# Hybrid attention and gMLP block on one core: the closing norm of the MLP's last eight blocks, worked half a row at a time

## The chip, the core and the metric

The kernel runs on one core of a Trainium2 chip. The metric is device microseconds of that core for one launch. Five engines work beside each other, each through its own queue in order: TensorE (PE in the profile, with its weight loads as PEld), VectorE (DVE), ScalarE (ACT), GpSimd (POOL) and SyncE (SP), which here only issues transfers.

## What is computed

The reference is one decoder layer on 2048 rows of 1024 channels, in float32: a norm, dilated window attention and a gated spatial mixer, their merge, a projection, a norm added to the input; then a squared-ReLU MLP with a norm before and after it. Only the very end matters here:

```python
def _rmsnorm(x, gain):
    xf = x.astype(jnp.float32)
    y = xf * lax.rsqrt(jnp.mean(xf * xf, axis=-1, keepdims=True) + EPS)
    return (y * gain.astype(jnp.float32)).astype(x.dtype)
...
h = _rmsnorm(x, norm_pre_mlp[layer])
a = jax.nn.relu(jnp.einsum('bsd,df->bsf', h, w_mlp_in[layer]))
y = jnp.einsum('bsf,fd->bsd', a * a, w_mlp_out[layer])
x = x + _rmsnorm(y, norm_post_mlp[layer])
```

So every row of y needs its sum of squares over 1024 channels, the reciprocal root of their mean, a product with the gain (`gfin`), a product with the root, and a sum with the row of x that went into the MLP (`x1`).

## The kernel before

**Tiles and stages.** Each float32 operand is split into a rounded high part and the rest (`split`, L70 for the high part, L78 for the rest), and each product is three matmuls (high-high, high-rest, rest-high). The second product of the MLP is the last stage, from 2139.5 us on. It runs over 64 steps n (`ysteps`): eight groups of the 4096 inner channels, and in each group eight blocks of 256 rows. Steps 56 to 63 are the last group, in which every block gets its final sums. A block is two parts of 128 rows (ci = 0 and 1), each with two halves of 512 channels (h = 0 and 1): four quarters (ci, h), which lie in two accumulators of 128 x 1024 (`acc`).

**Products.** A block is multiplied by a 2 x 2 scheme with seven products instead of eight, numbered 1, 2, 6, 7, 5, 4, 3 in their order (`yproduct`, L1529 and L1534). One product is six matmuls of 128x512. Products 1, 6, 7 and 4 collect in one bank (a), 2 in its own (b), 5 and 3 in a third (c). After each one VectorE adds the bank so far to a quarter (L1534), and the next product of the bank waits for that add. The quarters are complete after product 2 (quarter 0,0), 5 (1,1), 4 (1,0) and 3 (0,1). Three blocks of the last group (`PLAIN`) are multiplied plainly instead: eight products p0 to p7, two for each quarter, one add for each two (L1512 and L1516). In the text below "58's product 6" is product 6 of step 58.

**The order.** A list (`yorder`) lays the products of neighbouring steps into each other: in the window of step n stand, in this order, n's 1, (n-1)'s 7 and 5, n's 2 and 6, (n-1)'s 4 and 3. A plain block puts p0 to p3 in its window and p4 to p7 in the next. The other four engines do their work in the order in which the code issues it; nothing is rearranged. Behind the last product of step n (L1597) the sums and splits of step n+3's left operand begin (`sum_s`): a first split (ACT, then DVE), four sums on POOL (L1330 to L1333), and one and two windows' slots later a second and a third split. A plain step has only two splits, the second with its rest on POOL.

**The closing norm.** `finish(n)` starts right behind the last product of step n of the last group. It issues four loads of `x1` on SP's queue (L1438) into four places of their own, then four squares on ACT, each with a sum over 512 channels (L1442), and four products with the gain on POOL (L1443). Three slots later comes the reciprocal root (`rstd_act`, L119 to L129: nine small steps on ACT and one reciprocal on DVE), and at six and seven slots two and two instructions on DVE that multiply by the root and add `x1` (L1449), each followed by its store (L1450). The last step has its own functions (`finish_half`, `finish_row`, `load_final`); its `x1` goes into the two accumulators of step 56, and those four loads are issued behind the last product of step 62 ahead of step 62's own. At the very end stand a chain on DVE and ACT for the last 128 rows (L1480, `rstd_of` L102 to L113, L1487) and two stores.

Two late loads (L1588) bring two more quarters of the MLP's weights (`w2r_b`) for the plain blocks; they wait until POOL has read the buffers that they reuse, and are split on ACT and DVE (L1591).

Of the kernel before, what the change touches and what calls it, by code (L numbers as in the profile page):

```python
# [16 lines left out]
P = 128  # L17
S = 2048
D = 1024
# [22 lines left out]
def block_kernel(ctx, tc, a, out):  # L42
# [73 lines left out]
    def rstd_act(pl, ss, n, scale, tag):  # L116

        b, w, v, r, t = (pl.tile([P, n], F32, name=f"{o}_{tag}", tag=f"ra_{o}{n}") for o in "bwvrt")
        act.activation(b, ss[:, 1], AF.Identity, bias=eps, scale=scale)  # L119
# [3 lines left out]
        act.activation(w, v, AF.Copy, scale=-0.5)  # L123
        dve.reciprocal(r, r)
        act.activation(t, r, AF.Square)
        for k in range(n):
            act.activation(t[:, k:k + 1], t[:, k:k + 1], AF.Identity, bias=three_halves, scale=w[:, k:k + 1])
        for k in range(n):
            act.activation(r[:, k:k + 1], r[:, k:k + 1], AF.Copy, scale=t[:, k:k + 1])  # L129
        return r  # L130

    def dtile(shape, name):
        return dram.tile(shape, F32, name=name)
# [1296 lines left out]
    def finish(n):  # L1430

        g, half, i = ysteps[n]
        ss = sm.tile([P, 2, 2], F32, name=f"fs_{n}", tag="fs")
        rows = [(ci, h, half * HALF + ci * 512 + i * P, slice(h * 512, (h + 1) * 512)) for ci in range(2) for h in range(2)]
        x1 = {}
        for ci, h, t0, nsl in rows:
            x1[ci, h] = rx.tile([P, 512], F32, name=f"x1_{n}{ci}{h}", tag="xs", bufs=LEAD + 1)
            sp.dma_start(x1[ci, h], x1_d[t0:t0 + P, nsl])  # L1438
        for ci, h, t0, nsl in rows:
            junk = psum_any(f"jk_{n}{ci}{h}")  # L1440
            y = acc[half, i, ci][:, nsl]
            act.activation(junk, y, AF.Square, accum_out=ss[:, h, ci:ci + 1])  # L1442
            pool.tensor_mul(y, y, gfin[h])  # L1443
        yield
        r = rstd_act(sm, ss, 2, 1.0 / D, f"fin{n}")
        yield
        for m, (ci, h, t0, nsl) in enumerate(rows):
            y = acc[half, i, ci][:, nsl]
            dve.scalar_tensor_tensor(y, y, r[:, ci:ci + 1], x1[ci, h], op0=OP.mult, op1=OP.add)  # L1449
            sp.dma_start(out[t0:t0 + P, nsl], y)  # L1450
            if m == 1:
                yield

    fin_ss, fin_x1, fin_y, last_rows = {}, {}, {}, {}

    def finish_half(ci, h):

        n = FINAL
        g, half, i = ysteps[n]
        if not h:  # L1460
            fin_ss[ci] = sm.tile([P, 2, 1], F32, name=f"fe_{ci}", tag=f"fe{ci}")
        y = acc[half, i, ci][:, h * 512:(h + 1) * 512]
        junk = psum_any(f"jk_{n}{ci}{h}")
        act.activation(junk, y, AF.Square, accum_out=fin_ss[ci][:, h])
        fin_y[ci, h] = y
        if h:

            z = acc[blocks[1] + (ci,)][:, :512]
            fin_y[ci, h] = z
            dve.tensor_mul(z, y, gfin[h])  # L1470
        else:
            pool.tensor_mul(y, y, gfin[h])

    def finish_row(ci):
        n = FINAL
        g, half, i = ysteps[n]
        t0 = half * HALF + ci * 512 + i * P
        ss = fin_ss[ci]
        if ci:
            dve.tensor_add(ss[:, 0], ss[:, 0], ss[:, 1])  # L1480
            r = rstd_of(sm, ss[:, 0], 1, 1.0 / D, f"fin{n}{ci}")
        else:
            r = rstd_act(sm, ss, 1, 1.0 / D, f"fin{n}{ci}")
        yield
        for h in range(2):
            y, nsl = fin_y[ci, h], slice(h * 512, (h + 1) * 512)
            dve.scalar_tensor_tensor(y, y, r, fin_x1[ci, h], op0=OP.mult, op1=OP.add)  # L1487
            (act if ci and h else sp).dma_start(out[t0:t0 + P, nsl], y)
        yield

    def load_final():
        n = FINAL
        last_rows.update((ci, finish_row(ci)) for ci in range(2))
        g, half, i = ysteps[n]
        for ci, h in OUTPUTS:
            t0 = half * HALF + ci * 512 + i * P
            x1 = acc[blocks[0] + (ci,)][:, h * 512:(h + 1) * 512]
            sp.dma_start(x1, x1_d[t0:t0 + P, h * 512:(h + 1) * 512])
            fin_x1[ci, h] = x1

    def plain(n, k):

        g, half, b = ysteps[n]
        (ci, nh), t = OUTPUTS[k // 2], k % 2
        if not t:
            ybank[n, k // 2] = psum_any(f"y{k // 2}_{n}")
        p = ybank[n, k // 2]
        at_, name = ((0, 1), (3, 2))[ci][t], (("B11", "B21"), ("B12", "B22"))[nh][t]
        for m, q in enumerate((2 * g, 2 * g + 1)):
            s, w = st_[n][:, :, m, at_], w2_[q, name]  # L1510
            for o, (l, r) in enumerate(((0, 0), (0, 1), (1, 0))):
                pe.matmul(p, s[:, l], w[:, r], start=not t and not m and not o, stop=t == 1 and m == 1 and o == 2,  # L1512
                          skip_group_check=True)
        if t:
            an = acc[half, b, ci][:, nh * 512:(nh + 1) * 512]
            dve.tensor_add(an, an, p)  # L1516

    def yproduct(n, i):

# [32 lines left out]
    def at(k, gen):  # L1552
        todo.setdefault(k, []).append(gen)
# [4 lines left out]
    for k, (_, n, i) in enumerate(yorder):  # L1558
# [25 lines left out]
        if (n, i) == (PLAIN[0] - 3, 3):  # L1584

            for q in (NQ - 2, NQ - 1):
                w2r_[q] = r4.tile([P, 5, 512], F32, name=f"w2r_b{q}", tag="w2r", bufs=2)
                sp.dma_start(w2r_[q][:, 1], a["w_mlp_out"][2 * q][:, 512:])  # L1588
        if (n, i) == (PLAIN[0] - 2, 7):
            for q in (NQ - 2, NQ - 1):  # L1590
                op_w2(q, "B12", "dve")  # L1591
        if n == FINAL:
            if i[1] % 2:
                finish_half(*OUTPUTS[i[1] // 2])
            for at_, ci in ((4, 0), (6, 0), (7, 1), (7, 1)):
                if i[1] == at_:
                    next(last_rows[ci])  # L1597
        elif i in (3, ("p", 7)):
            m = n + 3
            if m < len(ysteps):  # L1600
# [3 lines left out]
                load_s(m + 1)  # L1604
                at(k + 6, st)
                at(k + 7, st)
            if n == FINAL - 1:
                load_final()
# [74 lines left out]
```

## Time and profile before

| | us |
|---|---|
| three timed runs | 2808.26, 2811.08, 2811.70 (median 2811.08) |
| profiled execution | 2814.08 |
| span of its instructions | 2812.4 |
| TensorE busy | 2722.6 (97%) |
| VectorE, ScalarE, GpSimd busy | 1568.7, 1061.8, 976.7 |
| granted TensorE clock, mean | 0.987 |

Times in the profile count from the first instruction of the span. A row of the timeline has the start, the length, engine, source line, operation, output and inputs by the program's names without buffer numbers, how many instructions it merges, and in brackets the idle time ahead of it with what ended it. A row of the list of waits has who waited for whom, the sum, the number of waits and the longest. In the profile `s` is the split left operand, `sraw` its raw form, `jk` the thrown-away output of a square, `T_spots` split weights, `x` a place for `x1`, and `acc`, `acc_yt`, `acc_gmlp`, `B_acc`, `acc_y`, `acc_xr` are the accumulators of the blocks in the order of the steps.

### The profile page before, as it was taken

How to read it: one execution, taken by the hardware profiler on the slowest of the kernel's cores; microseconds unless marked ns; L12 is line 12 of the kernel's file. 1: busy time of each engine (PE TensorE's matmuls, PEld its weight loads, DVE VectorE, ACT ScalarE, POOL GpSimd, SP SyncE). 2: the span in 40 equal slices, each digit the busy share in tenths (PEclk: the TensorE clock that was granted, in tenths of full speed). 3: DMA queues.
4: the chain of work that ended last, by engine and by line, in shares of the span. 5: the costliest groups of instructions: out<-in, count | busy, mean ns of one | idle time of the engine just before them, and what ended most of it. 6: DMA issues, size and time to landing. Idle time of an engine off the chain costs nothing.

```text
span 2812.4 us, 36260 instructions
## 1 busy us (share of the span) xinstructions
PE 2722.6 (97%) x13382; PEld 2280.1 (81%) x13382; DVE 1568.7 (56%) x2670; ACT 1061.8 (38%) x2164; POOL 976.7 (35%) x806
## 2 busy tenths in 40 slices
PE   8999999999999999999998999999999999999987
PEld 8889888988878888787787788888887778877765
DVE  5664552433443344555556644655437777777767
ACT  4212111244444322344444545655444323332334
POOL 0241341200000023312215423233224777666765
PEclk9999999999999999999999999999999999999998
DMA  7544455466666554555658433643443221222235
GB/s 252 178 147 162 158 152 186 129 183 196 197 218 191 176 174 139 182 194 158 179 172 282 145 116 120 208 144 119 121 127 100 88 79 57 83 83 85 88 101 200
DMA packets 298673, 426.61 MB, mean 152 GB/s; under 512 B 18560, under 2 KB 172416, under 8 KB 298496
## 3 DMA queue, kind: packets, MB, share of 16 engines
q1 hardware_dynamic: 210800, 373.17, 42.0%
q10 hardware_dynamic: 87696, 51.13, 6.0%
q8 instruction: 105, 1.72, 0.3%
q14 instruction: 72, 0.59, 0.1%
HBM read 283.52 MB, written 140.71 MB: 151 GB/s over the span
## 4 chain that ended last, share of the span: by engine, by line
PE 79%; POOL 8%; DVE 4%; DMA 4%; issue 2%; ACT 2%; SPq 1%; ACTq 0%; DVEq 0%; POOLq 0%
PE ab L993 9%; PE ya L1529 7%; PE ac L993 6%; PE aa L993 5%; POOL T_spots L78 4%; PE g L95 4%; PE g L97 4%; PE g L96 4%; PE yc L1529 4%; PE x L97 3%; PE x L96 3%; PE x L95 3%; PE o L97 2%; PE o L95 2%; PE o L96 2%
## 5 line engine op out<-in xcount | busy, mean ns | idle before, releaser
L1529 PE MATMUL ya<-T_spots,s 128*128 128x512 f32 x1377 | 341.4, 394 | 5.0 <-DVE acc L1537 3.0
L1529 PEld LDWEIGHTS ya<-T_spots,s 128*128 128x128 f32 x1377 | 259.9, 189 | 64.5 <-issue 5.4
L70 ACT ACTIVATE s<-sraw 128x768 fp32r<-128x768 f32 (+1 forms) x189 | 130.0, 699 | 376.2 <-POOL sraw L1331 207.2
L993 PE MATMUL aa<-B,A 128*128 128x512 f32 x768 | 187.1, 396 | 7.3 <-ACT xs L1007 5.6
L78 DVE TENSOR_TENSOR s<-sraw,s 128x512 fp32r<-128x512 f32 (+1 forms) x181 | 177.6, 1003 | 29.8 <-ACT s L70 29.5
L1529 PE MATMUL yc<-T_spots,s 128*128 128x512 f32 x684 | 181.3, 396 | 10.5 <-DVE acc L1534 6.2
L964 POOL TENSOR_TENSOR s<-w1r 128x512 f32<-128x512 f32 x32 | 43.5, 1361 | 395.1 <-DVE S L78 335.1
L993 PEld LDWEIGHTS aa<-B,A 128*128 128x128 f32 x768 | 145.4, 190 | 41.3 <-ACT xs L1007 6.0
L72 POOL TENSOR_SCALAR w_g<-w_g_r 128x1024 fp32r<-128x1024 f32 x32 | 33.6, 1049 | 411.6 <-PE g L97 352.5
L1529 PEld LDWEIGHTS yc<-T_spots,s 128*128 128x128 f32 x684 | 127.8, 189 | 44.2 <-POOL T_spots L78 11.1
L95 PE MATMUL x<-hT_a,wq 128*128 128x512 f32 x384 | 149.7, 390 | 0.0
L97 PE MATMUL x<-hT_a,wq 128*128 128x512 f32 x384 | 149.4, 389 | 0.0
L96 PE MATMUL x<-hT_a,wq 128*128 128x512 f32 x384 | 149.4, 389 | 0.0
L630 DVE TENSOR_REDUCE o<-po 128x256 f32<-128x512 f32 x48 | 33.2, 691 | 183.9 <-PE po L629 183.9
L78 POOL TENSOR_TENSOR T_spots<-w2r,T_spots 128x512 fp32r<-128x512 f32 x92 | 131.8, 1460 | 0.0
L70 ACT ACTIVATE hl<-r 128x512 fp32r<-128x512 f32 x48 | 30.4, 633 | 231.5 <-POOL r L275 86.7
L1330 POOL TENSOR_TENSOR sraw<-sraw 128x256 f32<-128x256 f32 x61 | 45.0, 738 | 186.5 <-DVE s L78 172.2
L95 PE MATMUL o<-wo,mg 128*128 128x512 f32 x256 | 101.4, 396 | 4.7 <-ACT mg L70 4.2
L95 PE MATMUL g<-hT_b,w_g 128*128 128x512 f32 x256 | 105.3, 412 | 0.0
L95 PE MATMUL g<-hT_a,w_g 128*128 128x512 f32 x256 | 104.8, 409 | 0.0
L792 POOL TENSOR_TENSOR g<-g,g 128x512 f32<-128x512 f32 x28 | 38.9, 1388 | 186.2 <-DVE g L790 186.0
L70 ACT ACTIVATE S<-w1r 128x512 fp32r<-128x512 f32 x96 | 60.0, 629 | 113.9 <-PE ac L993 68.1
(381 smaller groups left out, 7447.2 us busy)
## 6 DMA issues: line engine op xcount, KB each, us to landing
w1r<-in_w_mlp_in_dram SPq DMA_DIRECT2D x64, 512.0 KB, 3.7
sraw<-sd SPq DMA_DIRECT2D x128, 256.0 KB, 3.4
qk<-hl SPq DMA_DIRECT2D x24, 1024.0 KB, 5.3
qq<-qk SPq DMA_DIRECT2D x96, 256.0 KB, 4.9
w_g_r<-in_w_in_dram SPq DMA_DIRECT2D x32, 512.0 KB, 5.5
gated<-gt SPq DMA_DIRECT2D x64, 256.0 KB, 3.0
g<-gated SPq DMA_DIRECT2D x64, 256.0 KB, 4.4
w2r<-in_w_mlp_out_dram SPq DMA_DIRECT2D x16, 1024.0 KB, 5.7
```

The costliest lines, as they stand in the source:

```text
L70: act.activation(hi, src, AF.Copy)
L72: pool.tensor_scalar(hi, src, 1.0, 1.0, op0=OP.mult, op1=OP.mult)
L78: (pool if lo_eng == "pool" else dve).tensor_sub(lo, src, f32(hi))
L95: pe.matmul(ps, lh, rh, start=start, stop=False)
L96: pe.matmul(ps, lh, rl, start=False, stop=False)
L97: pe.matmul(ps, ll, rh, start=False, stop=stop)
L630: dve.tensor_reduce(ot[:, :, j * 64:(j + 1) * 64], po.rearrange("p (b h e) -> p b e h", b=4, h=2), axis=AX.X, op=OP.add)
L792: (dve if dt == KT - 1 else pool).tensor_add(parts[0], parts[0], parts[1])
L964: pool.tensor_add(s1, a21, a22)
L993: pe.matmul(p, w[:, l, k, :], h[:, r, k, :], start=i in (1, 6, 5) and not k and not n, stop=k == 3 and n == 2, skip_group_check=True)
L1330: pool.tensor_add(a22, a21, a22)
L1529: pe.matmul(p, s[:, l], w[:, r], start=i in (1, 2, 5) and not m and not o, stop=m == 1 and o == 2, skip_group_check=True)
```

## The change

Each quarter's square and product with the gain are issued at once behind the add that completes it (`end_half`), in plain blocks after p1, p3, p5 and p7. `finish(n)` keeps only the reciprocal root, whose first part (up to the square root) is now issued one slot behind the block's last product and the rest one slot later, and the two pairs of closing instructions, at four and five slots. Their order in a block of seven products is (0,0), (1,1), (1,0), (0,1). `x1` is loaded behind the first completed quarter of its own block: for step 56 into places of its own, for 57 and 58 into the unused parts of the two late weight buffers, and for n from 59 on into the accumulators of step n-3, once these are stored. The plain blocks are now 59, 61 and 63 instead of 58, 60 and 63. The split of the two late weight quarters stands one step later.

```diff
+        yield r
         dve.reciprocal(r, r)
...
-    PLAIN = [n for n in range(len(ysteps)) if n >= len(ysteps) - len(blocks) and n % len(blocks) in (2, 4, 7)]
+    PLAIN = [n for n in range(len(ysteps)) if n >= len(ysteps) - len(blocks) and n % len(blocks) in (3, 5, 7)]
...
+    def load_x1(n):
+        for ci, h, t0, nsl in places_of(n):
+            if n == FIRST_END:
+                t = rx.tile([P, 512], F32, name=f"x1_{n}{ci}{h}", tag="xs", bufs=LEAD + 1)
+            elif n < FIRST_END + 3:
+                t = wb_[n - FIRST_END - 1][:, (0, 2, 3, 4)[2 * ci + h]]
+            else:
+                t = acc[blocks[n - FIRST_END - 3] + (ci,)][:, nsl]
+            sp.dma_start(t, x1_d[t0:t0 + P, nsl])
...
+        act.activation(junk, y, AF.Square, accum_out=ss_[n][:, h, ci:ci + 1])
+        if n == FINAL and h:
             z = acc[blocks[1] + (ci,)][:, :512]
             dve.tensor_mul(z, y, gfin[h])
+            y = z
         else:
             pool.tensor_mul(y, y, gfin[h])
...
+        rows = [rows[k] for k in ((0, 1, 2, 3) if n in PLAIN else (0, 3, 2, 1))]
+        for k in (0, 2):
+            end(n, r, 0, rows[k:k + 2], (sp, sp))
+            yield
...
             dve.tensor_add(an, an, p)
+            end_half(n, ci, nh)
...
+        if n >= FIRST_END and i in (2, 5, 4, 3):
+            end_half(n, ci, nh)
...
-        if (n, i) == (PLAIN[0] - 2, 7):
+        if (n, i) == (FIRST_END + 1, 7):
             for q in (NQ - 2, NQ - 1):
                 op_w2(q, "B12", "dve")
+        if n >= FIRST_END and i in (2, ("p", 0)):
+            load_x1(n)
...
-                next(f)
-                for d in (1, 3, 4) if n == FINAL - 1 else (3, 6, 7):
+                at(k + 1, f)
+                for d in (2, 3, 4) if n == FINAL - 1 else (2, 4, 5):
```

Lines after the first hunk stand higher by one to six in the changed kernel (L1534 becomes L1537, L1449 becomes L1471). The order of every engine is the same in both programs up to step 56.

**ACT, around the splits for step 62.** `s_62` and `s_63` are the split operands of those steps, `jk_6010` is the square of quarter (1,0) of step 60. Before:

```order
L1442 ACTIVATE jk_5911_22296,fs_59_22278<-acc_yt4_17862 128x512
L127 ACTIVATE t_fin59_22325<-t_fin59_22325,edge_87,w_fin59_22322 128x1 x2
L129 ACTIVATE r_fin59_22324<-r_fin59_22324,t_fin59_22325 128x1 x2
L70 ACTIVATE s_62_22268<-sraw_62_22166 128x2x256
L70 ACTIVATE s_62_22268<-sraw_62_22166 128x2x2x128
L70 ACTIVATE s_63_22385<-sraw_63_22275 128x2x256
L1442 ACTIVATE jk_6000_22397,fs_60_22388<-acc_yt5_17863 128x512
L1442 ACTIVATE jk_6001_22400,fs_60_22388<-acc_yt5_17863 128x512
L1442 ACTIVATE jk_6010_22403,fs_60_22388<-B22_acc_17855 128x512
L1442 ACTIVATE jk_6011_22406,fs_60_22388<-B22_acc_17855 128x512
```

And now:

```order
L1458 ACTIVATE jk_6011_22339,fs_60_22249<-B22_acc_17855 128x512
L1458 ACTIVATE jk_6100_22350,fs_61_22349<-B22_acc_17855 128x512
L1458 ACTIVATE jk_6010_22375,fs_60_22249<-B22_acc_17855 128x512
L70 ACTIVATE s_62_22287<-sraw_62_22183 128x2x256
L1458 ACTIVATE jk_6001_22387,fs_60_22249<-acc_yt5_17863 128x512
L70 ACTIVATE s_62_22287<-sraw_62_22183 128x2x2x128
L70 ACTIVATE s_63_22392<-sraw_63_22294 128x2x256
L1458 ACTIVATE jk_6101_22402,fs_61_22349<-B22_acc_17855 128x512
L119 ACTIVATE b_fin60_22405<-fs_60_22249,edge_87 128x2
L121 ACTIVATE v_fin60_22407<-fs_60_22249,b_fin60_22405 128x1 x2
```

The second and third split for step 62 stood together, ahead of all four squares of step 60; now each stands behind a square of step 60, that of the quarter which product 4 or 3 of step 60 completes, and the square of quarter (0,1) stands between the two.

**DVE, the same place.** `yc_60` and `ya_60` are the banks of step 60, and an L1537 row with `ya_62` is the add of 62's product 1. Now:

```order
L1471 SCALAR_TENSOR_TENSOR acc_yt3_17861<-acc_yt3_17861,r_fin59_22307,acc1_17856 128x512 x2
L1471 SCALAR_TENSOR_TENSOR acc_yt4_17862<-acc_yt4_17862,r_fin59_22307,acc0_17702 128x512 x2
L1537 TENSOR_TENSOR B22_acc_17855<-B22_acc_17855,ya_60_22206 128x512
L78 TENSOR_TENSOR s_62_22287<-sraw_62_22183,s_62_22287 128x2x256
L1537 TENSOR_TENSOR acc_yt5_17863<-acc_yt5_17863,yc_60_22331 128x512
L78 TENSOR_TENSOR s_62_22287<-sraw_62_22183,s_62_22287 128x2x2x128
L78 TENSOR_TENSOR s_63_22392<-sraw_63_22294,s_63_22392 128x2x256
L1518 TENSOR_TENSOR B22_acc_17855<-B22_acc_17855,y1_61_22357 128x512
L1537 TENSOR_TENSOR B22_acc_17855<-B22_acc_17855,ya_62_22415 128x512
L125 RECIPROCAL r_fin60_22408<-r_fin60_22408 128x2
```

The four closing instructions of step 59 stand ahead of the add for 60's product 4, and behind that add the rests of three splits alternate with adds, up to the add for 62's product 1, for which 62's product 6 waits. Before, the same add stood behind the rests of the splits and step 59's closing instructions as well, but no rest there came behind a square of that window.

**DVE, at the end.** `y3_63` is the bank of the last two products. Before:

```order
L124 RECIPROCAL r_fin62_22621<-r_fin62_22621 128x2
L1470 TENSOR_TENSOR acc_yt0_17857<-acc_y11_17865,gfin1_17852 128x512
L124 RECIPROCAL r_fin630_22647<-r_fin630_22647 128x1
L1516 TENSOR_TENSOR acc_xr0_17866<-acc_xr0_17866,y2_63_22637 128x512
L1449 SCALAR_TENSOR_TENSOR B22_acc_17855<-B22_acc_17855,r_fin62_22621,x1_6200_22591 128x512
L1449 SCALAR_TENSOR_TENSOR B22_acc_17855<-B22_acc_17855,r_fin62_22621,x1_6201_22593 128x512
L1449 SCALAR_TENSOR_TENSOR acc_y10_17864<-acc_y10_17864,r_fin62_22621,x1_6210_22595 128x512
L1449 SCALAR_TENSOR_TENSOR acc_y10_17864<-acc_y10_17864,r_fin62_22621,x1_6211_22597 128x512
L1487 SCALAR_TENSOR_TENSOR acc_y11_17865<-acc_y11_17865,r_fin630_22647,acc1_17856 128x512
L1487 SCALAR_TENSOR_TENSOR acc_yt0_17857<-acc_yt0_17857,r_fin630_22647,acc1_17856 128x512
L1516 TENSOR_TENSOR acc_xr0_17866<-acc_xr0_17866,y3_63_22672 128x512
```

And now:

```order
L1462 TENSOR_TENSOR acc_yt0_17857<-acc_y11_17865,gfin1_17852 128x512
L125 RECIPROCAL r_fin62_22600<-r_fin62_22600 128x2
L1518 TENSOR_TENSOR acc_xr0_17866<-acc_xr0_17866,y2_63_22607 128x512
L1471 SCALAR_TENSOR_TENSOR B22_acc_17855<-B22_acc_17855,r_fin62_22600,acc_yt3_17861 128x512
L1471 SCALAR_TENSOR_TENSOR acc_y10_17864<-acc_y10_17864,r_fin62_22600,acc_yt4_17862 128x512
L125 RECIPROCAL r_fin630_22623<-r_fin630_22623 128x1
L1471 SCALAR_TENSOR_TENSOR acc_y10_17864<-acc_y10_17864,r_fin62_22600,acc_yt4_17862 128x512
L1471 SCALAR_TENSOR_TENSOR B22_acc_17855<-B22_acc_17855,r_fin62_22600,acc_yt3_17861 128x512
L1471 SCALAR_TENSOR_TENSOR acc_y11_17865<-acc_y11_17865,r_fin630_22623,acc_yt5_17863 128x512
L1471 SCALAR_TENSOR_TENSOR acc_yt0_17857<-acc_yt0_17857,r_fin630_22623,acc_yt5_17863 128x512
L1518 TENSOR_TENSOR acc_xr0_17866<-acc_xr0_17866,y3_63_22647 128x512
```

The instructions are the same ones, in nearly the same places; what moved is their second input. Step 62's `x1` is now in the accumulators of step 59 (`acc_yt3`, `acc_yt4`), loaded a window and more ahead, where it was in `x1_62` places whose loads are issued behind the last stores. On SP the loads of `x1` for step 63 stood just ahead of those for step 62 and behind the stores of steps 60 and 61:

```order
L1450 DMA out_0_dram<-B22_acc_17855 128x512 x4
L1498 DMA acc1_17856<-x1d_79 128x512 x2
L1498 DMA acc0_17702<-x1d_79 128x512 x2
L1438 DMA x1_6200_22591<-x1d_79 128x512
L1438 DMA x1_6201_22593<-x1d_79 128x512
```

Now they stand behind the stores of step 60 alone:

```order
L1472 DMA out_0_dram<-acc_yt5_17863 128x512
L1448 DMA acc_yt3_17861<-x1d_79 128x512 x2
L1448 DMA acc_yt4_17862<-x1d_79 128x512 x2
L1448 DMA acc_yt5_17863<-x1d_79 128x512 x2
L1448 DMA B22_acc_17855<-x1d_79 128x512 x2
L1472 DMA out_0_dram<-B22_acc_17855 128x512 x5
```

What moved is the stores of step 61, now behind these loads.

More of the change, by code (lines that the diff above doesn't have):

```diff
@@ L1428, in block_kernel, with places_of @@
     begun, ybank, left, todo = set(), {}, {}, {}
-    def finish(n):
+    FIRST_END = len(ysteps) - len(blocks)
+    x1_, ss_, y_, wb_, last_rows = {}, {}, {}, {}, {}
+    def places_of(n, ci=None):
         g, half, i = ysteps[n]
[L1433 to L1452, printed above, removed]
@@ L1454, in block_kernel @@
-    fin_ss, fin_x1, fin_y, last_rows = {}, {}, {}, {}
-    def finish_half(ci, h):
-        n = FINAL
+        return [(c, h, half * HALF + c * 512 + i * P, slice(h * 512, (h + 1) * 512)) for c in range(2) for h in range(2)
+                if ci in (None, c)]
+    def load_x1(n):
[7 more added lines that the diff above has]
+            sp.dma_start(t, x1_d[t0:t0 + P, nsl])
+            x1_[n, ci, h] = t
@@ L1474, in finish_row, with finish @@
+    def finish(n):
+        r_ = rstd_act(sm, ss_[n], 2, 1.0 / D, f"fin{n}")
+        r = next(r_)
+        yield
+        next(r_)
+        yield
+        rows = places_of(n)
+        rows = [rows[k] for k in ((0, 1, 2, 3) if n in PLAIN else (0, 3, 2, 1))]
+        for k in (0, 2):
+            end(n, r, 0, rows[k:k + 2], (sp, sp))
+            yield
     def finish_row(ci):
         n = FINAL
-        g, half, i = ysteps[n]
-        t0 = half * HALF + ci * 512 + i * P
-        ss = fin_ss[ci]
+        ss = ss_[n][:, :, ci:ci + 1]
@@ L1482, in finish_row @@
         else:
-            r = rstd_act(sm, ss, 1, 1.0 / D, f"fin{n}{ci}")
-        yield
[L1485 to L1499, printed above, removed]
+            r_ = rstd_act(sm, ss, 1, 1.0 / D, f"fin{n}{ci}")
+            r = next(r_)
+            yield
+            next(r_)
+            yield
+        end(n, r, ci, places_of(n, ci), (sp, act if ci else sp))
+        yield
     def plain(n, k):
```

33 lines of the change are left out of this document (17 added, 16 removed).

## The prediction

> **What bounds the kernel now.** First the page's totals, then for the last stretch the list of waits, the windows with the granted clock, and the timeline.
>
> ```profile
> span 2812.4 us, 36260 instructions
> PE 2722.6 (97%) x13382; PEld 2280.1 (81%) x13382; DVE 1568.7 (56%) x2670; ACT 1061.8 (38%) x2164; POOL 976.7 (35%) x806
> ```
>
> TensorE sets the time everywhere, and up to step 56 the programs agree. So only the last 126 us can change: the last group's 63 products, and what follows them. TensorE's timeline (start, length, line, what, and in brackets the idle time ahead with its releaser) at the first of them, and at two that wait:
>
> ```profile
> 2686.38 2.90 PE L1529 MATMUL ya<-T_spots,s 128*128 128x512 f32 x12
> ...
> 2711.67 2.93 PE L1529 MATMUL yc<-T_spots,s 128*128 128x512 f32 x6 [6.20 <-DVE acc L1534]
> ...
> 2773.51 1.65 PE L1529 MATMUL ya<-spot,s 128*128 128x512 f32 x3 [4.71 <-DVE B_acc L1534]
> ```
>
> The list of waits from 2660 to the end (sum, number, longest) has four for TensorE that count, and two that stand behind the first:
>
> ```profile
> PE yc L1529 <- DVE acc L1534: 6.2, 1, 6.2
> PE ya L1529 <- DVE B_acc L1534: 4.7, 1, 4.7
> PE ya L1529 <- DVE acc_yt L1534: 2.7, 1, 2.7
> PE yc L1529 <- POOL T_spots L78: 0.7, 1, 0.7
> ACT T_spots L70 <- DMA w2r_b<-in_w_mlp_out_dram: 10.2, 2, 8.7
> DVE T_spots L78 <- ACT T_spots L70: 7.3, 2, 5.9
> ```
>
> The 6.2 is 56's product 3, the 2.7 is 59's product 6 and the 4.7 is 62's product 6. Each costs more than its length. The windows behind the three waits and the last stretch (window: length, then busy time and instructions of PE, PEld, DVE, ACT and POOL, granted clock, DMA):
>
> ```profile
> 2711.70:2717.00 5.30, 5.30 (x13) 4.14 (x14) 3.35 (x5) 2.37 (x6) 0.86 (x2) 0.50 0.62 189
> 2735.00:2743.50 8.50, 8.46 (x24) 6.69 (x25) 5.56 (x10) 2.93 (x8) 1.27 (x1) 0.63 0.85 297
> 2773.50:2778.80 5.30, 5.29 (x13) 4.14 (x14) 2.59 (x5) 2.60 (x10) 2.46 (x3) 0.50 0.57 172
> 2778.80:2797.40 18.60, 18.31 (x79) 14.37 (x77) 13.49 (x19) 11.07 (x40) 12.33 (x9) 1.00 0.59 208
> ```
>
> In the last window 79 matmuls take 18.31, so one product of six takes 1.37 with its share of overlap. At a clock of 0.50 half of 5.3 is lost, 2.65, and at 0.63 it is 0.37 x 8.5 = 3.1. Losses: 6.2 + 2.65, 2.7 + 3.1, 4.7 + 2.65, 0.7, about 23; with 63 x 1.37 = 86.3 and small waits the products end at 2797.4. The tail:
>
> ```profile
> 2791.59 5.79 PE L1512 MATMUL y<-T_spots,s 128*128 128x512 f32 x24 [0.27 <-DVE B_acc L1534]
> 2801.14 1.41 DVE L1449 SCALAR_TENSOR_TENSOR B_acc<-B_acc,r_fin,x 128x512 f32<-128x512 f32 x2 [2.75 <-DMA x<-x1d]
> 2802.47 1.41 DVE L1449 SCALAR_TENSOR_TENSOR acc_y<-acc_y,r_fin,x 128x512 f32<-128x512 f32 x2
> 2805.12 0.68 DVE L1516 TENSOR_TENSOR acc_xr<-acc_xr,y 128x512 f32<-128x512 f32 x1
> ```
>
> TensorE ends at 2797.38, but VectorE makes the last add at 2805.12: step 62's closing instructions hold its queue for a transfer. From that add to the end of the span it is 2812.4 - 2805.12 = 7.28, a chain on VectorE and ScalarE and two stores that the change leaves as it is. With T for the start of 62's product 6 (2773.51), the span ends at T + 38.9.
>
> **Part by part.** Squares, gain products, small steps, closing instructions, loads and stores stay as many as they were; what changes is where they stand. So the cost lies in waits, priced with these rows (VectorE, POOL, ScalarE):
>
> ```profile
> 2715.51 0.96 DVE L78 TENSOR_TENSOR s<-sraw,s 128x768 fp32r<-128x768 f32 x1 [0.19 <-ACT s L70]
> 2724.17 0.69 DVE L1534 TENSOR_TENSOR acc_yt<-acc_yt,ya 128x512 f32<-128x512 f32 x1 [2.04 <-PE ya L1529]
> 2724.77 0.69 DVE L78 TENSOR_TENSOR s<-sraw,s 128x512 fp32r<-128x512 f32 x1
> 2728.63 3.48 DVE L1449 SCALAR_TENSOR_TENSOR acc<-acc,r_fin,x 128x512 f32<-128x512 f32 x2
> 2732.04 1.75 DVE L78 TENSOR_TENSOR s<-sraw,s 128x512 fp32r<-128x512 f32 x1
> 2738.61 2.73 DVE L1449 SCALAR_TENSOR_TENSOR acc_yt<-acc_yt,r_fin,x 128x512 f32<-128x512 f32 x4
> 2697.58 8.42 POOL L78 TENSOR_TENSOR T_spots<-w2r,T_spots 128x512 fp32r<-128x512 f32 x6
> 2716.60 0.73 POOL L1330 TENSOR_TENSOR sraw<-sraw 128x256 f32<-128x256 f32 x1 [4.44 <-DVE s L78]
> 2726.86 6.38 POOL L1443 TENSOR_TENSOR acc_yt<-acc_yt,gfin 128x512 f32<-128x512 f32 x4 [2.05 <-ACT jk L1442]
> 2747.47 2.58 POOL L1443 TENSOR_TENSOR acc_yt<-acc_yt,gfin 128x512 f32<-128x512 f32 x2
> 2716.00 0.58 ACT L1442 ACTIVATE jk<-acc 128x512 f32<-128x512 f32 x1
> 2716.52 0.19 ACT L1442 ACTIVATION_READ_ACCUMULATOR jk<-acc 128x1 f32 x1
> 2717.96 0.30 ACT L119 ACTIVATE b_fin<-fs,edge 128x2 f32<-128x2 f32 x1
> 2718.91 0.19 ACT L123 ACTIVATE w_fin<-v_fin 128x2 f32<-128x2 f32 x1
> 2720.87 0.20 ACT L125 ACTIVATE t_fin<-r_fin 128x2 f32<-128x2 f32 x1 [1.77 <-DVE r_fin L124]
> 2721.68 0.47 ACT L129 ACTIVATE r_fin<-r_fin,t_fin 128x1 f32<-128x1 f32 x2
> 2722.05 1.14 ACT L70 ACTIVATE s<-sraw 128x512 fp32r<-128x512 f32 x2
> ```
>
> A closing instruction takes 2.73 / 4 = 0.68 alone and 3.48 / 2 = 1.74 while POOL multiplies by the gain; a rest 0.69 or 1.75; a gain product 2.58 / 2 = 1.29 alone and 6.38 / 4 = 1.60 beside VectorE; a square with its sum 2716.71 - 2716.00 = 0.71; a high part 0.57; the first part of a root 2719.10 - 2717.96 = 1.14, its second 2722.15 - 2720.87 = 1.28. One link "add, square behind it, high part behind that, rest" costs 0.69 + 0.71 + 0.57 and 0.69 to 1.75: 2.7 to 3.7. Such links are what the change lays between the splits and the add on which TensorE waits.
>
> *Step 56.* The late weights' split leaves the place ahead of the add, so the 6.2 goes. What is late next is POOL: its six rests of T_spots would end at 2697.58 + 8.42 = 2706.0, now one gain product (1.29) stands between them, 2707.3, and 56's product 3, due at 2711.67 - 6.20 = 2705.5, loses about 1.1 in its last third. The clock should hold.
>
> *58's product 6* (a product of the new order) is due four products later, at 2713.2. It waits for 58's product 1 to be added, and that stands behind the rests of two splits. POOL's four sums for 58 begin at 2707.3, two are there at 2708.8; high part 2709.4, rest 2710.1, add of 56's product 3 2710.7, its square 2711.45, high part 2712.0, two rests beside gain products (2 x 1.75) 2715.5, add 2716.2. A wait of 3.0, and 2.7 at the low clock behind it.
>
> *60's product 6.* Fifteen products later TensorE is there at 2716.2 + 15 x 1.37 + 2.7 = 2739.5. VectorE gets there later. From the add of 57's product 3 at 2727.3: two squares and two high parts 2.15, rest of 768 columns (0.96 alone) beside POOL 1.5, add, reciprocal and second part of the root 1.9, four closing instructions of step 57 of which two lie beside POOL 4.9, add 0.65, square and high part 1.3, rest 1.2, add 0.6, square and high part 1.3, rest 1.45, then a rest and two adds 1.85. Sum 18.8, so 2746.1: 6.65 of waiting.
>
> *62's product 6.* Due at 2746.1 + 23.25 = 2769.35. Step 59's closing instructions start four slots behind its last product, 13.5 after 60's product 6 (three slowed products 6.8, four more 5.5, an add and a hop): 2759.6. Four beside POOL 6.0, add 0.65, then as above 1.3, 1.4, 0.6, 1.3, 1.4 and a rest and two adds 1.85: 14.5, so **2774.1**, 0.6 later than now. The waits lost at 56 and 59 come back at 58, 60 and 62: 0.7 + 1.1 + 5.7 + 9.35 + 7.45 = 24.3 where 23 and small ones stood.
>
> *Tail.* Fifteen products take 15 x 1.37 + 2.7 = 23.25 as before. `x1` of step 62 is issued with the stores of step 60 and not at the end; loads near here:
>
> ```profile
> x<-x1d SPq DMA_DIRECT2D x28, 256.0 KB, 4.8
> sraw<-sd SPq DMA_DIRECT2D x18, 256.0 KB, 3.7
> ```
>
> Issued from T + 7 on behind step 60's stores, at 4.8 each, it is there by about T + 15, ahead of the closing instructions at T + 22; that cover of 7 hides it. What is late next is the chain of roots: square of 63's quarter (0,1) at T + 20.2, reciprocals at 21.3 and 25.3, a gain product until 25.7, two closing instructions, last add at T + 26.9; with 7.28 the end is at **T + 34.1**, 4.8 earlier than T + 38.9.
>
> *Sum.* 2774.1 + 34.1 = 2808.2, 4.2 under the span. The profiled execution took 2814.08, 1.7 more than its span and 3.0 more than the median: 2814.08 - 4.2 = 2809.9 for it, and **2806.8** against the median of 2811.08.
>
> *Both ends.* What I priced between alone and beside POOL spans, for steps 58, 60 and 62, two rests, then three rests and four closing instructions twice. All alone: 2.1 + 1.8 + 2.2 + 1.6 + 3.3 = 11.0 earlier, 2796. All beside POOL: 2.0 + 2.1 + 1.9 + 1.0 = 7 later, 2814. I took about half beside POOL, since POOL is busy 12.33 of the last 18.6.
>
> The row of 1.74 also meets a rule. The Trainium skill, "SBUF — State Buffer", section "SBUF: two separate sides", calls the port pair of VectorE and GpSimd an exclusive lock: who starts first keeps it for the whole instruction and the other blocks. By that a closing instruction begun with a gain product ends after 1.29 + 0.68 = 1.97, not 1.74; over some 11 of them 2.5 more, 2809.3, an estimate from that page. It speaks against the change; the measured 1.74 is nearer to the lock than to none, and I keep it.
>
> A second rule bears on the 3.0 wait at 58. The Trainium skill, "TensorE: Matmul & The Clock Gate", Part 1, lets the clock fall after an idle window of about 3.4 us. By that page 58's wait could leave the clock, and the end would come 2.7 earlier, 2804.1, an estimate. The trace differs: 2.71 of waiting was followed by a clock of 0.63.
>
> **Rivals.** *A, faster:* gain products come one at a time and end before VectorE closes, so the eight closing instructions run at 0.68: 2.2 + 3.3 = 5.5 earlier, 2801.3. For it: POOL has idle time (4.44 ahead of 2716.60). Against: they are issued just behind the adds where VectorE is busiest. *B, slower:* at 58, 60 and 62 one more link shows, because the square of the neighbour's quarter, too, stands ahead of the high part on ScalarE and VectorE has nothing left to do meanwhile. Price 0.69 + 0.71 + 0.57 + 1.75 = 3.7 at each, 11.1 in all: 2817.9. It decides from the point where the add ahead of that square ends later than POOL's second sum, which in the walk is nearest at 62. For it: the splits were free of squares. Against: VectorE's queue is late itself, so part of a link hides. *C, no gain in the tail:* the loads for 62 queue behind stores that wait for VectorE, and the new place for `x1` gives nothing: +4.8, 2811.6. For it: SP's queue is in order; against: 7 us of cover.
>
> **How the numbers follow.** The walk as made 0.43 (own range 2803 to 2810), A 0.27, B 0.22, C 0.08. A measurement of this kernel can tell about 0.2%, 5.6 us: faster is under 2805.5, slower over 2816.7. Faster: 0.17 of the walk and 0.25 of A, 0.42. Slower: 0.16 of B and 0.02 of C, 0.18. Same: 0.40. Outside 2797 to 2818 I leave A's far end and B's, 0.08 and 0.1.
>
> **What would show it.** Right: in the list of waits the 6.2 and the wait for `x1` at the end are gone, TensorE waits at 58, 60 and 62 for VectorE's add, 3, 6.7 and 4.7 long, the low clock behind each; the last add comes 26.9 after 62's product 6. Wrong: a wait of TensorE elsewhere, or T outside 2768 to 2780; closing instructions at 0.68 speak for A, a wait of VectorE for a high part ahead of 62's add of over 3 for B, a wait for `x1` for C.

## The result, and the profile after

The changed kernel took 2809.98 us (median of 14 runs, 2806.74 to 2816.36), the kernel before 2811.55 beside it (14 runs, 2805.80 to 2814.63). The ratio is 1.0000, 95% interval 0.9991 to 1.0008. The time lies inside the forecast's range, but the gain does not show: the medians differ by 1.6 us where 4.3 were forecast, the interval reaches from 2.5 us faster to 2.2 us slower, and the forecast's ratio of 0.9985 lies outside it. The profiled execution took 2810.95, with a span of 2809.2.

In the changed kernel the squares stand at L1458, the products with the gain at L1465 and the closing instructions at L1471, 22 lines on from L1449 and not one to six as the text ahead has it. The waits of TensorE from 2660 to the end (sum, number, longest), and one of VectorE, which stands first, in the kernel before and in the changed one:

```profile
DVE s L78 <- ACT s L70: 1.9, 4, 0.9
```

```profile
DVE s L78 <- ACT s L70: 15.3, 10, 3.5
...
PE ya L1532 <- DVE acc_yt L1537: 7.1, 4, 3.4
...
PE ya L1532 <- DVE B_acc L1537: 4.0, 2, 3.4
...
PE yc L1532 <- POOL T_spots L78: 1.6, 3, 0.7
```

The 6.2 at 56 is gone, and so is the wait for `x1`. In their place stand many shorter ones: VectorE now waits ten times for ScalarE's high parts, 15.3 us in all where it waited 1.9, and TensorE waits for VectorE. TensorE's timeline shows where:

```profile
2687.03 2.90 PE L1532 MATMUL ya<-T_spots,s 128*128 128x512 f32 x12
...
2717.17 1.62 PE L1532 MATMUL ya<-spot,s 128*128 128x512 f32 x3 [2.61 <-DVE acc_yt L1537]
...
2732.24 1.65 PE L1532 MATMUL ya<-T_spots,s 128*128 128x512 f32 x6 [1.38 <-DVE acc_gmlp L1537]
...
2739.43 3.03 PE L1514 MATMUL y<-T_spots,s 128*128 128x512 f32 x12 [1.44 <-DVE acc_gmlp L1537]
...
2747.27 1.29 PE L1532 MATMUL ya<-spot,s 128*128 128x512 f32 x3 [3.43 <-DVE acc_yt L1537]
...
2774.70 1.42 PE L1532 MATMUL ya<-spot,s 128*128 128x512 f32 x3 [3.43 <-DVE B_acc L1537]
```

These are the start of the last group, then product 6 of 58, 60 and 62 with a wait each, and between 58 and 60 two more waits of 1.4 (and one of 0.53) that the walk had put at 60. The 1.6 behind POOL is three short waits at 56: 0.71 at its product 5, as before the change, and 0.64 and 0.28 at its product 3. The tail on VectorE:

```profile
2796.93 0.75 DVE L1471 SCALAR_TENSOR_TENSOR B_acc<-B_acc,r_fin,acc_yt 128x512 f32<-128x512 f32 x1 [0.57 <-ACT r_fin L130]
...
2801.99 0.68 DVE L1518 TENSOR_TENSOR acc_xr<-acc_xr,y 128x512 f32<-128x512 f32 x1
```

Step 62's first closing instruction now waits for its root, not for a transfer, and the last add comes at 2801.99.

Executions of one program start the last group at other times (2683.7 to 2689.5 in the profiles here), so all that follows is counted from its first row in the timeline (S), over 62's product 6 (T) and the last add (A), to the end of the span. All come from rows of the timelines; those that carry the argument stand below, and the first line is from the rows of the prediction.

| profile | S to T | T to A | A to end | S to end |
|---|---|---|---|---|
| before | 87.1 | 31.6 | 7.3 | 126.0 |
| before, again | 84.1 | 30.6 | 7.3 | 122.0 |
| before, a third time | 84.1 | 31.6 | 7.3 | 123.0 |
| changed | 87.7 | 27.3 | 7.2 | 122.2 |
| changed, again | 87.6 | 27.6 | 7.2 | 122.4 |
| before with `x1` early | 84.9 | 29.8 | 7.3 | 121.9 |
| changed, squares behind the splits | 83.6 | 25.9 | 7.3 | 116.8 |
| changed, no gain products on POOL | 75.7 | 24.1 | 7.2 | 107.0 |

### The profile page after: what moved, and what is told of

The parts are those of the page before. It is cut to its first block, busy times and chain, and to the rows that moved or that the text cites. A ratio compares the mean times of both kernels' runs of the same rounds, so it can differ in the third digit from the quotient of the medians.

```text
span 2809.2 us, 36263 instructions
## 1 busy us (share of the span) xinstructions
PE 2721.7 (97%) x13382; PEld 2277.5 (81%) x13382; DVE 1574.9 (56%) x2670; ACT 1062.9 (38%) x2164; POOL 979.4 (35%) x806
## 4 chain that ended last, share of the span: by engine, by line
PE 77%; POOL 8%; DVE 5%; DMA 4%; issue 3%; ACT 2%; SPq 0%; ACTq 0%; DVEq 0%; POOLq 0%
PE ab L994 9%; PE ya L1532 7%; PE ac L994 6%; PE aa L994 5%; POOL T_spots L78 4%; PE g L95 4%; PE g L97 4%; PE g L96 4%; PE yc L1532 3%; PE x L95 3%; PE x L97 3%; PE x L96 3%; PE o L97 2%; PE o L95 2%; PE o L96 2%
## 5 line engine op out<-in xcount | busy, mean ns | idle before, releaser
L70 ACT ACTIVATE S<-w1r 128x512 fp32r<-128x512 f32 x96 | 60.2, 631 | 111.9 <-PE ac L994 66.3
```

Of the source, the lines that this page charges most:

```text
L70: act.activation(hi, src, AF.Copy)
```

## The experiments

My theory after the result: the walk of the changed kernel is right, and the base was wrong, since the one profile of before had an unusually long last group. The rival: the gain is really about 4 and hidden by scatter, or the tail's gain is not the transfer's.

### Both kernels once more

```
(no edit: the changed kernel; the kernel before, twice)
```

> The changed kernel once more, as it is. Theory (the last group is worked out alike in every execution, and the scatter of the times comes from ahead of it): 122.2 us within 0.5 from the start of the last group to the end, with waits at 58, 60 and 62 of 2.6, 3.4 and 3.4; time 0.05% to 0.15% under the kernel before. Rival (the gain seen in one pair of profiles is chance): waits or length differ by 2 us or more, time equal.

> The kernel before once more, as it is. In two profiles of the same program up to 62's product 6 (the kernel before, and the one with only the transfer of x1 moved) the way from the start of the last group to that product took 87.1 and 84.9 us. Theory (the low clock behind a wait costs another amount in each execution, and the profile of before was a long one): 84.5 to 86 here, with waits of 5.5 to 6.5 at 56 and 2.7 at 59, and 124 to 125 for the last group. Rival (the first profile is typical): 87 and 126.

> The kernel before a third time. Theory (after a wait of 2.5 to 3 us the clock sometimes falls and sometimes holds, so the last group of this kernel scatters): 121.5 to 124.5 us for the last group, with what is lost behind the wait at 59 anywhere from 0 to 3. Rival (126 is the rule and the second profile of 122 the exception): 125 to 127.

The changed kernel again: 122.4 from S to the end with waits of 2.69, 3.42 and 3.43 at 58, 60 and 62, as expected, and 2810.03 (12 runs) against 2811.34 (33 runs), ratio 0.9997 (0.9987 to 1.0006). This interval, too, includes no change. The kernel before, second and third profile, with the window of 8.5 us behind the wait at 59 first (length; PE, PEld, DVE, ACT, POOL busy; granted clock; DMA):

```profile
2735.80:2744.30 8.50, 8.49 (x37) 7.01 (x38) 6.74 (x11) 5.76 (x18) 2.32 (x3) 1.00 0.87 307
```

```profile
2688.22 2.90 PE L1529 MATMUL ya<-T_spots,s 128*128 128x512 f32 x12
...
2712.72 2.93 PE L1529 MATMUL yc<-T_spots,s 128*128 128x512 f32 x6 [5.42 <-DVE acc L1534]
...
2735.81 0.97 PE L1529 MATMUL ya<-spot,s 128*128 128x512 f32 x3 [2.92 <-DVE acc_yt L1534]
...
2772.36 1.65 PE L1529 MATMUL ya<-spot,s 128*128 128x512 f32 x3 [4.77 <-DVE B_acc L1534]
```

```profile
2802.94 0.68 DVE L1516 TENSOR_TENSOR acc_xr<-acc_xr,y 128x512 f32<-128x512 f32 x1
```

```profile
2731.60:2740.10 8.50, 8.50 (x37) 7.02 (x38) 6.71 (x11) 5.79 (x18) 2.34 (x3) 1.00 0.89 308
```

```profile
2684.00 2.90 PE L1529 MATMUL ya<-T_spots,s 128*128 128x512 f32 x12
...
2731.59 0.96 PE L1529 MATMUL ya<-spot,s 128*128 128x512 f32 x3 [3.06 <-DVE acc_yt L1534]
...
2768.12 1.65 PE L1529 MATMUL ya<-spot,s 128*128 128x512 f32 x3 [4.72 <-DVE B_acc L1534]
```

```profile
2795.75 1.42 DVE L1449 SCALAR_TENSOR_TENSOR B_acc<-B_acc,r_fin,x 128x512 f32<-128x512 f32 x2 [2.38 <-POOL acc_xr L1472]
...
2799.73 0.68 DVE L1516 TENSOR_TENSOR acc_xr<-acc_xr,y 128x512 f32<-128x512 f32 x1
```

S to T is 84.1 in both, 3.0 less than in the profile that I had worked from. Behind waits of 2.92 and 3.06 at 59 the clock stayed at 1.00 in 8.5 us; in the first profile it was 0.63 behind 2.71. That is 0.37 x 8.5 = 3.1, and the wait at 56 was 5.4 and not 6.2 (in part given back: both executions wait 1.05 and 1.08 at 61's product 6, where the first did not wait). The expectation for the second profile, 84.5 to 86 and a group of 124 to 125, was still too long; the one for the third, 121.5 to 124.5, held. So 126.0 was the long one of three, and the changed kernel, whose VectorE sets T, comes to 87.6 and 87.7 in both profiles.

### The transfer alone

```diff
+            if n == FINAL - 1:
+                x1[ci, h] = early_x1[ci, h]
+                continue
...
+        if (n, i) == (FINAL - 1, 2):
+            load_early()
+            load_final()
...
-            if n == FINAL - 1:
-                load_final()
```

> The kernel before, with only the x1 of steps 62 and 63 loaded early (behind 62's product 2, that of 62 into the accumulators of step 59). Measure: time from the start of the last group (56's product 1) to the end of the span, 126.0 us before and 122.2 in the changed kernel. Theory (the tail's term is the transfer): 62's product 6 stays where it was, the wait of 2.75 for x1 goes, the roots are late next, so 123.3, 2.7 less. Rival (the tail gains only when the squares come earlier, too): VectorE still waits for the roots, 125 to 126.

```profile
2689.47 2.90 PE L1542 MATMUL ya<-T_spots,s 128*128 128x512 f32 x12
...
2736.93 0.97 PE L1542 MATMUL ya<-spot,s 128*128 128x512 f32 x3 [2.87 <-DVE acc_yt L1547]
...
2774.33 1.65 PE L1542 MATMUL ya<-spot,s 128*128 128x512 f32 x3 [4.72 <-DVE B_acc L1547]
```

```profile
2798.48 0.16 DVE L124 RECIPROCAL r_fin<-r_fin 128x1 f32<-128x1 f32 x1 [1.83 <-ACT r_fin L122]
...
2799.15 1.41 DVE L1452 SCALAR_TENSOR_TENSOR B_acc<-B_acc,r_fin,acc_yt 128x512 f32<-128x512 f32 x2
2800.47 2.42 DVE L1452 SCALAR_TENSOR_TENSOR acc_y<-acc_y,r_fin,acc_yt 128x512 f32<-128x512 f32 x2
...
2804.13 0.68 DVE L1529 TENSOR_TENSOR acc_xr<-acc_xr,y 128x512 f32<-128x512 f32 x1
```

2809.32 (12 runs), ratio 0.9994 (0.9986 to 1.0002), so not clear of no change either; but this edit alone stands no worse than the whole change, which took 2810.03 beside it. The wait goes, and T to A is 29.8 where three profiles of before have 31.6, 30.6 and 31.6: 1.5 less on average, not the 2.7 that I expected. Part of it is lost again in the last row of closing instructions: two take 2.42 where they took 1.41, because they now run beside POOL's last gain product (2800.32 to 2801.68) instead of behind it. S to T is 84.9, near the 84.1 of the two later profiles of before. Of the tail's gain of 3.8 (from 31.3 on average to 27.4) less than half is the transfer. The rest goes with the order: here the closing instructions still stand behind the reciprocal for step 63, for which VectorE waits 1.83, and in the changed kernel they stand ahead of it, so that the first starts 22.2 after T and not 24.8. No run tests that order by itself.

### The square between two splits

```diff
         if n >= FIRST_END and i in (2, 5, 4, 3):
-            end_half(n, ci, nh)
+            ends.append((n, ci, nh))
...
         for gen in todo.pop(k, ()):
             next(gen, None)
+        while ends:
+            end_half(*ends.pop(0))
```

(and the same for the plain blocks.)

> The changed kernel, with each quarter's square and gain product issued behind the split that stands in the same slot instead of ahead of it. Theory (the links 'add, square, high part, rest' set when TensorE goes on at 60 and 62): each of two links loses a square of 0.65 at 60 and at 62, so 62's product 6 comes 2.3 to 2.6 earlier and the last group takes 119.8 instead of 122.2. Rival (VectorE's own queue, with rests and closing instructions beside POOL, sets it): 122 to 122.5.

2804.21 (10 runs), ratio 0.9974 (0.9965 to 0.9983): **faster than both**: at the medians it takes 7.1 us less than the kernel before and 5.8 less than the changed kernel beside it. VectorE ahead of 62's product 6, first in the changed kernel, then in this one, both from the add for 60's product 4:

```profile
2766.15 0.68 DVE L1537 TENSOR_TENSOR B_acc<-B_acc,ya 128x512 f32<-128x512 f32 x1
2768.14 1.36 DVE L78 TENSOR_TENSOR s<-sraw,s 128x512 fp32r<-128x512 f32 x1 [1.31 <-ACT s L70]
2769.43 0.68 DVE L1537 TENSOR_TENSOR acc_yt<-acc_yt,yc 128x512 f32<-128x512 f32 x1
2771.42 1.95 DVE L78 TENSOR_TENSOR s<-sraw,s 128x512 fp32r<-128x512 f32 x2 [1.31 <-ACT s L70]
...
2773.88 0.68 DVE L1537 TENSOR_TENSOR B_acc<-B_acc,ya 128x512 f32<-128x512 f32 x1
```

```profile
2763.62 0.67 DVE L1537 TENSOR_TENSOR B_acc<-B_acc,ya 128x512 f32<-128x512 f32 x1
2764.22 0.68 DVE L78 TENSOR_TENSOR s<-sraw,s 128x512 fp32r<-128x512 f32 x1
2764.82 0.67 DVE L1537 TENSOR_TENSOR acc_yt<-acc_yt,yc 128x512 f32<-128x512 f32 x1
2765.61 3.07 DVE L78 TENSOR_TENSOR s<-sraw,s 128x512 fp32r<-128x512 f32 x2
...
2769.20 0.67 DVE L1537 TENSOR_TENSOR B_acc<-B_acc,ya 128x512 f32<-128x512 f32 x1
```

In the changed kernel VectorE stands still twice for 1.31: ScalarE takes its square of the add just made, then the high part, and only then VectorE has a rest to work on. ScalarE's rows for the first of the two:

```profile
2766.86 0.60 ACT L1458 ACTIVATE jk<-B_acc 128x512 f32<-128x512 f32 x1 [5.03 <-DVE B_acc L1537]
...
2767.49 0.62 ACT L70 ACTIVATE s<-sraw 128x512 fp32r<-128x512 f32 x1
```

With the square behind, both waits are gone, and from the first add to the end of the last it is 6.2 instead of 8.4. What remains at 60 and 62 is shorter:

```profile
2745.91 0.94 PE L1532 MATMUL ya<-spot,s 128*128 128x512 f32 x3 [1.28 <-ACT jk L1458]
...
2770.02 0.93 PE L1532 MATMUL ya<-spot,s 128*128 128x512 f32 x3 [1.26 <-DVE r_fin L125]
```

The gain went beyond the 2.4 expected, with 4.0 from S to T and 1.5 from T to A. Of the 4.0, 0.7 are there at 60's product 6, 2.2 lie between the start of step 59's closing instructions and the add for 62's product 1, and 1.2 come because those closing instructions start 12.1 after 60's product 6 and not 13.3. The low clock is spared at 60 and 62: over 5.3 us behind the waits of 1.3 it was 1.00, where the changed kernel's two profiles had 0.50 to 0.68 behind waits of 3.4.

Is it the square, or POOL's gain product that moved with it?

```diff
     def end_half(n, ci, h):
+        end_square(n, ci, h)
+        if n == FINAL:
+            end_gain(n, ci, h)
+        else:
+            ends.append((n, ci, h))
```

(the products follow behind the split, the squares stay.)

> The changed kernel with only the gain products issued behind the split of the same slot; the squares stay ahead of it. Theory (it is the square in ScalarE's queue that lengthens the links): 62's product 6 as in the changed kernel, waits of 3.4 at 60 and 62, last group 121.5 to 122.5. Rival (the place of the gain product in POOL's queue did it): the waits fall to 1.3 and the last group to 117.

```profile
2774.57 1.08 PE L1543 MATMUL ya<-spot,s 128*128 128x512 f32 x3 [3.39 <-DVE B_acc L1548]
```

One time, 2810.78, with a span of 2809.1 and 122.6 for the group, 0.1 over what I expected; the waits at 60 and 62 are those of the changed kernel, and VectorE's two waits of 1.31 are still there. So the product's place alone does nothing. The squares alone were not moved, so that they suffice without the products is read from the rows and not tested.

### The plain blocks and the late split, put back

```diff
-... n % len(blocks) in (3, 5, 7)]
+... n % len(blocks) in (2, 4, 7)]
...
-        if (n, i) == (FIRST_END + 1, 7):
+        if (n, i) == (FIRST_END, 7):
```

> The changed kernel with the plain blocks at 58, 60 and 63 and the late weights' split one step earlier, as before the change. Theory (the wait of 6.2 at 56 goes because that split moves): it comes back, about 6 at 56's product 3 and 2.7 at the low clock behind it, waits at 58 and 60 go, one at 59 comes: last group 125 to 127. Rival (which blocks are plain makes no difference): 122.

> The changed kernel with the split of the late weights one step earlier, where the kernel before had it. Theory (that place made the wait of 6.2 at 56, and what is removed there is given back at 58): the wait at 56 is back with 6 to 7, the one of 2.6 at 58 is gone or under 1, and the last group takes 122 to 125 where 122.2 stood, so far less than 6 more. Rival (the 6 add fully): 128.

With both edits 2812.08 (12 runs), ratio 1.0000 (0.9991 to 1.0009), and 124.6 for the group, just under the 125 to 127 expected. TensorE's waits from 2680 on, the largest of which are at 56 (7.1), 59 (3.3) and 61 (3.7), are:

```profile
PE yc L1532 <- DVE acc L1537: 7.1, 1, 7.1
PE ya L1532 <- DVE B_acc L1537: 5.0, 2, 3.7
PE ya L1532 <- DVE acc_yt L1537: 3.3, 1, 3.3
```

With the second edit alone (one time, 2811.83), at 56's product 3 and then at 60's product 6:

```profile
2712.29 2.93 PE L1532 MATMUL yc<-T_spots,s 128*128 128x512 f32 x6 [6.88 <-DVE acc L1537]
...
2748.20 0.94 PE L1532 MATMUL ya<-spot,s 128*128 128x512 f32 x3 [3.42 <-DVE acc_yt L1537]
```

The wait at 56 is back with 6.88, the one at 58 is gone (its product 6 starts at 2722.05 without one), and 60 waits 3.42 as in the changed kernel. From the start of the group (2686.31) to the end (2810.1) it is 123.8, only 1.6 more than 122.2. So removing 6.2 at 56 was worth under 2 in these profiles, one of the edit against two without it: VectorE and ScalarE are late at 60 and 62 whatever TensorE has saved before.

### Contention, and closings later

```diff
-        else:
-            pool.tensor_mul(y, y, gfin[h])
```

> The changed kernel without POOL's products with the gain: the output lacks that factor except where VectorE multiplies it. Theory (VectorE's instructions beside those products set when TensorE goes on): closing instructions take 0.75 or less each, rests 0.7, the waits at 60 and 62 shrink from 3.4 to under 1.5, the last group takes 112 to 117. Rival (the links through ScalarE's squares set it, and contention is beside the path): the waits stay over 2.5, last group 120 to 122.

One time, 2792.43; 107.0 for the group. VectorE's rests of 512 columns and step 59's closing instructions from 2715 on (busy, mean ns), first in the changed kernel, then here:

```profile
L78 DVE TENSOR_TENSOR s<-sraw,s 128x512 fp32r<-128x512 f32 x7 | 8.4, 1219 | 5.3 <-ACT s L70 5.3
L1471 DVE SCALAR_TENSOR_TENSOR acc_yt<-acc_yt,r_fin,acc 128x512 f32<-128x512 f32 x4 | 5.7, 1484 | 0.0
```

```profile
L78 DVE TENSOR_TENSOR s<-sraw,s 128x512 fp32r<-128x512 f32 x6 | 4.0, 690 | 5.2 <-ACT s L70 5.2
L1469 DVE SCALAR_TENSOR_TENSOR acc_yt<-acc_yt,r_fin,acc 128x512 f32<-128x512 f32 x4 | 3.1, 843 | 0.0
```

1.22 falls to 0.69 and 1.48 to 0.84. S to T is 11.9 shorter, where the prediction's bound "all alone" had 11.0. The group fell below the 112 to 117 expected, though 60 still waits 2.07 and not under 1.5; 62 does not wait. Between S and T VectorE ran 79 instructions in both kernels and was busy 66.4 us in the changed one and 53.5 here, so the shortening is in the length of its instructions and not in shorter waits. (The squares are still in their places, so contention and links add on one path, and neither alone is the cause.) To spare the contention and keep the result:

```diff
-        else:
+        elif n >= FINAL - 1:
             pool.tensor_mul(y, y, gfin[h])
...
+            if n < FINAL - 1:
+                dve.scalar_tensor_tensor(y, y, r[:, ci - k:ci - k + 1], gfin[h], op0=OP.mult, op1=OP.mult)
+                dve.tensor_add(y, y, x1_[n, ci, h])
```

> The kernel with the squares behind the splits, and without POOL's gain products for steps 56 to 61: there each closing takes two instructions on VectorE, one that multiplies by the root and the gain and one that adds x1. It computes what the reference does. Theory (what POOL's products cost is VectorE's instructions beside them, 1.75 instead of 0.7): four closings of two instructions take 4 x 1.35 = 5.4, as four did beside POOL, while rests and sums run at their own length, so waits at 60 and 62 go to 1 or less, last group 112 to 115, time 0.35% to 0.45% under the kernel before. Rival (VectorE's number of instructions sets it): no better than 117.

2815.08 (11 runs), ratio 1.0015 (1.0006 to 1.0024): slower, with 126.8 for the group where 112 to 115 were expected. The waits at product 6 of 60 and 62 do go, but others of up to 2.56 stand ahead of them; S to T is 84.3, no better than 83.6, and behind T TensorE stops where it did not before:

```profile
2780.85 2.93 PE L1536 MATMUL ya<-T_spots,s 128*128 128x512 f32 x6 [4.19 <-DVE B_acc L1541]
```

Eight closing instructions of step 60, from 2772.00 on, stand ahead of the add that it waits for, which starts at 2780.12. The rival held: what POOL no longer takes, VectorE's longer queue takes. Last, the closings moved back to six and seven slots in the kernel with the squares behind:

```diff
-                for d in (2, 3, 4) if n == FINAL - 1 else (2, 4, 5):
+                for d in (2, 3, 4) if n == FINAL - 1 else (2, 6, 7):
```

> The kernel with the squares behind the splits, and in addition the closing instructions of each step at six and seven slots behind its last product, where the kernel before had them, instead of four and five. Theory (four closing instructions in a row of 5.3 to 5.7 ahead of the adds are what TensorE waits for now): they move into VectorE's idle gaps between the rests, the waits of 2.4 and 1.3 go, last group 113 to 116 where 116.8 stood. Rival (they then stand among the rests ahead of the adds for which 60's and 62's product 6 wait): waits there of 3 or more, last group 117 to 121.

```profile
2745.03 1.12 PE L1532 MATMUL ya<-spot,s 128*128 128x512 f32 x3 [3.46 <-ACT jk L1458]
...
2770.45 1.62 PE L1532 MATMUL ya<-spot,s 128*128 128x512 f32 x3 [3.04 <-DVE r_fin L125]
```

2805.52 (11 runs), ratio 0.9975 (0.9966 to 0.9984), 118.6 for the group. The rival held here too: two waits between 58 and 60 shrink, and 3.46 and 3.04 stand at 60 and 62 instead of 1.3. T is the same.

## Why the prediction was right or wrong

**The walk was right** in what waits for what, and near in its sizes. At 56 it had 1.1 behind POOL, measured 0.64 + 0.28. At 58 a wait of 3.0, measured 2.61 and 2.69. 60's product 6 was put 59.7 after the start of the group (2746.1 - 2686.4) and came at 60.2; of the 6.65 of waiting 3.43 stood at 60 itself and 0.5 + 1.4 + 1.4 a few products ahead. At 62 it had 4.7, measured 3.43 with 0.54 and 0.52 ahead. 62's product 6 was put at 87.7 and came at 87.7. T to the last add was 26.9, measured 27.3 and 27.6, and the span 2808.2 against 2809.2, of which 0.65 is the later start of the group. The low clock behind 58, put at 2.7, was less, and came to nothing in the second profile; it did not matter, since VectorE sets the next start.

**The step that failed** is the last one: "2809.9 for it, and 2806.8 against the median". I took the 3.0 by which the profiled execution lay above the median for something that both kernels have, and moved the forecast down by it. It sat in the last group itself (126.0 against 122.0 and 123.0): the low clock behind the wait at 59 and a longer wait at 56, in a stretch that the change replaces. Without that shift the walk gives 2808.2 + 1.7 = 2809.9, and 2809.98 was measured. That this fits to 0.1 is luck: the 14 runs spread over 9.6 us, and the start of the group over 5.8 in the profiles. Put as terms: ahead of T the change costs some 2.6 (87.6 against 84.1, 84.1, 84.9 and 87.1, on average 85.1), not 0.6; the tail gives 3.8, not 4.8; the difference is 1.2, and the medians have 1.6 and 1.3. All of these are smaller than the scatter, so that the change gains anything is not shown.

**The low clock** was mis-sized as a constant: 2.65 to 3.1 behind each wait. It differs between executions. Four executions of one program up to there (the kernel before, and x1 early), with waits of 2.71, 2.87, 2.92 and 3.06 at 59, had 0.63, 0.80, 1.00 and 1.00 in the next 8.5 us. The row with 0.80 (x1 early):

```profile
2736.90:2745.40 8.50, 8.47 (x30) 6.79 (x31) 6.43 (x10) 4.19 (x12) 1.73 (x2) 0.80 0.85 305
```

The Trainium skill, "TensorE: Matmul & The Clock Gate", Part 1 (The HAM clock gate), says that the clock is judged by a free-running window that does not start with the work; the scatter agrees with that. Its length of about 3.4 us as the least idle time does not: 0.63 followed 2.71, and without the gain products 0.68 over 5.3 us followed 2.07. I had set the rule against one row; it takes several executions to see which part holds.

**The tail** was right: "that cover of 7 hides it" held, the wait for `x1` is gone and the root is late next. Its gain was put 1 too high: the last add came 0.5 later than in the walk, and the 31.6 of the first profile is 0.3 over the mean of three. The prediction did not say how much of it is the transfer; alone that is worth 1.5, since POOL's last product then falls beside the closings.

**The rivals.** A did not happen: step 59's closings still took 1.48 each beside POOL; its price was no exaggeration, as the kernel without the products shows. B did not add a link, but its mechanism, the square ahead of the high part, was already on the path at 60 and 62, twice each; moving squares and gain products behind the splits took 5.4 off the group. C did not happen.

**Open:** in the third profile of before the profile names POOL's product, not the transfer, ahead of step 62's first closing (2.38). The code has no such dependence (62's own products were done), the product ended 0.03 ahead of it; whether `x1` had landed by then is not to be seen.

## What to carry to other kernels

A difference between a walked kernel and one profile carries that execution's luck: profile the kernel before more than once, and ask in which stretch its distance from the median lies before shifting a forecast by it. Work that is put "right behind its input" goes behind the work that the bound engine's feeder waits for: here moving the squares and gain products behind the splits of the same slots was worth 5.8 us, where the whole change shows no gain. And a wait that is removed ahead of another late engine is given back there.

## What the runs showed of the hardware

The clock behind a wait of 2.7 to 3.1 us was anything from 0.63 to 1.00 over the next 8.5 us in executions of one program; behind waits of 1.3 (squares behind the splits) it stayed at 1.00 over 5.3 us in both windows. In between it went either way: 0.68 behind 2.39 (squares behind the splits) and behind 2.07 (no gain products), 1.00 behind 2.01 in the same execution, each over some 5.3 us. In the changed kernel itself 58's waits of 2.61 and 2.69 were followed by 0.71 and 1.00 over 5.3 us, and the end moved by 0.2 only, because VectorE, not TensorE, set the next start: in the second, TensorE waits 1.34 for it right behind the first products of that stretch, where the first profile does not wait.
